# Hybrid Fourier and RWKV-7 layer: the pair scores as one sequence beside twelve column tiles, and eight modulation blocks in pieces

## The chip, the cores and the metric

The kernel runs on one core of a Trainium2 chip. The metric is the device time of the whole kernel in microseconds (us), as a median of runs; lower is better. Engines are named as in the profile: PE multiplies matrices (PEld is its weight load), DVE, ACT and POOL work on vectors, and DMA queues (SP's above all) move data between HBM and the on-chip memory. All data is float32.

## The reference

One layer of a backbone: a modulated norm, one input projection whose columns feed a Fourier mix and eight bidirectional RWKV-7 heads, an output projection, a second modulated norm and a gated MLP with a 3x3 grid convolution. There are 1024 latent tokens and 256 context tokens, and the width is 1024. What this change touches is the modulation, the projection and what the heads' scan reads:

```python
mod_x = jax.nn.silu(c) @ ada_w[l] + ada_b[l]
mod_c = jax.nn.silu(c_ctx) @ ada_w[l] + ada_b[l]
sh1, sc1, g1, sh2, sc2, g2 = [m[:, None, :] for m in jnp.split(mod_x, 6, axis=-1)]
...
h = modulate(rms_norm(x, norm1_g[l]), sh1, sc1)
hc = modulate(rms_norm(ctx, norm1_g[l]), sh1c, sc1c)
...
u = h @ w_in
...
rkv = conv1d_centred(u[..., :3 * RWKV_W], conv_w)
r, k, v = jnp.split(rkv, 3, axis=-1)
...
decay = jnp.exp(-jnp.exp(-jax.nn.softplus(-w_lora) - 0.5))
a = jax.nn.sigmoid((a0 + jnp.einsum("btdr,drc->btdc", ad, a2)).astype(jnp.float32))
kk = (k * k_k).astype(jnp.float32).reshape(b, t, N_HEADS, HEAD)
kk = kk * lax.rsqrt(jnp.sum(kk * kk, axis=-1, keepdims=True) + KK_EPS)
...
def step(s, inp):
    r_t, k_t, v_t, kk_t, a_t, w_t = inp
    sa = jnp.einsum("dbhij,dbhj->dbhi", s, kk_t)
    s = (s * w_t[..., None, :] - sa[..., :, None] * (kk_t * a_t)[..., None, :]
         + v_t[..., :, None] * k_t[..., None, :])
    y = jnp.einsum("dbhij,dbhj->dbhi", s, r_t) if readout else None
    return s, y
```

The kernel computes the scan in chunks of 64 tokens. The scores of a chunk are products of its decayed k, kk, a and r rows, and do not need v.

## The kernel before

**Column tiles.** The projection is computed in tiles of 128 columns, each over all tokens. A float32 product is made of three fast matmuls: weights and activations are split into a high and a low part (`whi`, `wlo`, `hTh`, `hTl`; L188, L189), and whi x hTh, whi x hTl and wlo x hTh are added up. A tile has eight steps over the 1024 rows of the weights (`product_part`, L197), each of six matmuls of 512 columns for the latent tokens (`plat`); k and v tiles then have 24 matmuls of 256 columns for the context tokens (`pctx`). Tile numbers m: r is 0 to 3, k is 4 to 7, v is 8 to 11, one for each pair of heads; 12 is wd (decay), 13 is ad (learning rate), 14 is gd (gate).

**Modulation.** silu(c) times the 1024 x 6144 modulation matrix is made in twelve blocks of 512 columns. Each block loads 2 MB (`load_ad`, two buffers `ad`), runs 32 matmuls on the 32-column `sc32` (`ada_rows`, L283, 64 in the profile since a float32 matmul takes two passes), copies the sums on ACT (`br`, L286) and, where they are needed by column, transposes them on PE (`ada_cols`, L292). The first norm needs four blocks, which come first. The other eight (gate 1, shift 2, scale 2 into `g1`, `sh2`, `G2`, and gate 2 into `modrow`) are needed only behind the scan.

**First stage.** `stage0` normalizes the tokens in three blocks (512, 512 and 256 tokens), and after each runs its part of the tiles 12 and 13.

**Stage 1a.** Then the tiles k, v and r of pair 0 and the tile gd. Behind each tile, `tick(1000)` runs all side work to its end, and two of the eight modulation blocks follow.

**Stage 1b.** A pair's work is the generator `pair(p)`: ten units, which are five blocks of 256 tokens, the context block first, in two directions. Per block, `lora` loads the rows of wd and ad (`wa`, L521) and of k, kk, v and r (`kvb`, L524), which went to DRAM as `kvd`, runs four matmuls (L533) and tanh (L536). Per unit, `parts` makes `kd`, `bk` and `x8` on ACT, POOL and DVE (L554 to L575), `scores` runs 8 matmuls (16 passes, L617), a masked copy on DVE (L619), 8 transposes (L627) and a store to `xd` (L631); `bonus` (L581 to L584) follows each latent block's second unit. Behind a k tile, `norms` makes kk: a square on ACT (L460), three matmuls that sum over heads, a logarithm (L464), an exponential (L466), a product on DVE (L467). Behind a v tile, `turns` transposes v in six pieces (L493) and stores them.

**Order.** These generators stand in a round-robin list `sides`. After each step of a tile over the latent tokens, `tick(rate)` with rate 2 advances two of them by one yield; `paced` holds a tile's matmuls behind the instruction that the tick four before gave. So the written order is the order on the engines, up to what the tile framework's priorities move. Pair p runs beside the tiles r, k and v of pair p+1, and pair 3 beside two Fourier tiles. After the three tiles `drain(g)` runs the pair to its end without tiles. Four PSUM banks `aux` serve lora, scores, transposes, norms and turns, and the context part of the tiles.

## Time and profile before

| | |
|---|---|
| median of three runs | 1780.15 us (1778.44 to 1785.54) |
| the profiled execution | 1789.06 us |
| its span, first to last instruction | 1787.3 us |
| PE busy | 1543.1 us, 86% of the span |
| PE weight loads | 1253.2 us, beside the matmuls |
| DVE busy | 1145.7 us, 64% |
| ACT busy | 678.6 us, 38% |
| POOL busy | 511.1 us, 29% |
| mean granted PE clock | 0.91 |
| read from and written to HBM | 178.52 MB and 66.33 MB |

Busy times are shares of the whole span, and the stages differ much from each other, so a stage has to be read by itself. Rows of the trace have a start or a count, the engine, the line in the kernel, the operation and its tiles (out<-in); in brackets stands the idle time of the engine ahead of the instruction, and what ended it. A row of busy time by stretch has the stretch in us from the span's start, its length, for each engine the busy time with the number of instructions, and then the granted PE clock (1.00 is full speed), the busy share of the DMA engines and the GB/s that they moved. PE busy at a low clock counts for less work than at a high one.

### The profile page before, as it was taken

The numbers are of one execution on the slowest core, as the hardware profiler recorded it, in microseconds if no ns is written. First come the engines' busy times: TensorE is split into PE (matmuls) and PEld (weight loads), VectorE is DVE, ScalarE is ACT, GpSimd is POOL, SyncE is SP. The second block draws the span as 40 slices with busy tenths as digits, with TensorE's granted clock in tenths as the row PEclk, the third lists the DMA queues.
The fourth block names the chain that finished last, engine by engine and source line by source line (L and its number), as shares of the span: only waits on it lengthen the run. The fifth ranks groups of instructions, "written<-read, shape, count | busy, mean of one in ns | idle before, by whom it ended". The sixth has DMA issues, their size and how long they took to land. (4 is left out here: it accounts for less than half of the span.)

```text
span 1787.3 us, 28924 instructions
## 1 busy us (share of the span) xinstructions
PE 1543.1 (86%) x11642; PEld 1253.2 (70%) x11642; DVE 1145.7 (64%) x1624; ACT 678.6 (38%) x1165; POOL 511.1 (29%) x443
## 2 busy tenths in 40 slices
PE   3896788888987766868888899999999999899996
PEld 2785566666766556657677788888888887687685
DVE  3611364748477754849355769999999999714613
ACT  3431345555543223321455542222222223434533
POOL 0021343535232114121211412222222223355354
PEclk7898798989986857869998999999999999899998
DMA  8348475757578589985671031111111113544542
GB/s 302 143 167 274 141 247 168 236 182 253 183 198 195 101 132 196 171 190 114 151 160 50 16 123 47 48 47 48 49 55 50 48 48 105 205 138 128 190 130 95
DMA packets 177750, 246.80 MB, mean 138 GB/s; under 512 B 52278, under 2 KB 115392, under 8 KB 177616
## 3 DMA queue, kind: packets, MB, share of 16 engines
q1 hardware_dynamic: 171440, 234.44, 45.9%
q0 software_dynamic: 6176, 10.51, 2.5%
q8 instruction: 92, 1.51, 0.4%
q14 instruction: 42, 0.34, 0.1%
HBM read 178.52 MB, written 66.33 MB: 137 GB/s over the span
## 5 line engine op out<-in xcount | busy, mean ns | idle before, releaser
L189 POOL TENSOR_TENSOR wlo<-wraw,whi 128x1024 fp32r<-128x1024 f32 x105 | 253.7, 2417 | 694.8 <-ACT whi L188 694.8
L1186 DVE SCALAR_TENSOR_TENSOR conv<-u,c_fcw,conv 128x945 f32<-128x945 f32 (+2 forms) x344 | 411.4, 1219 | 36.3 <-ACT conv L1179 20.9
L188 ACT ACTIVATE whi<-wraw 128x1024 fp32r<-128x1024 f32 x123 | 129.4, 1052 | 312.7 <-issue 166.7
L197 PE MATMUL u<-h2l,whi 128*128 128x512 f32 x672 | 207.2, 389 | 0.0
L197 PE MATMUL u<-h2h,wlo 128*128 128x512 f32 x672 | 207.1, 389 | 0.0
L197 PE MATMUL u<-h2h,whi 128*128 128x512 f32 x672 | 207.0, 389 | 0.0
L189 DVE TENSOR_TENSOR al<-act,ah 128x256 fp32r<-128x256 f32 (+1 forms) x88 | 62.4, 713 | 139.4 <-ACT ah L188 139.2
L197 PEld LDWEIGHTS u<-h2h,wlo 128*128 128x128 f32 x672 | 126.2, 188 | 26.1
L197 PEld LDWEIGHTS u<-h2l,whi 128*128 128x128 f32 x672 | 126.2, 188 | 26.1
L197 PEld LDWEIGHTS u<-h2h,whi 128*128 128x128 f32 x672 | 126.2, 188 | 26.0
L1243 PE MATMUL e<-wlo,ah 128*128 128x512 f32 x264 | 103.1, 391 | 2.8 <-POOL wlo L189 2.8
L1243 PE MATMUL e<-whi,al 128*128 128x512 f32 x264 | 103.1, 390 | 0.0
L197 PE MATMUL plat<-hTh,whi 128*128 128x512 f32 x272 | 99.8, 449 | 1.6 <-ACT whi L188 1.1
L188 ACT ACTIVATE ah<-act 128x256 fp32r<-128x256 f32 (+1 forms) x88 | 45.8, 523 | 140.3 <-PE e L1243 99.3
L197 PE MATMUL plat<-hTl,whi 128*128 128x512 f32 x272 | 91.7, 417 | 0.0
L197 PE MATMUL plat<-hTh,wlo 128*128 128x512 f32 x272 | 90.6, 412 | 1.0 <-POOL wlo L189 1.0
L887 POOL COPY WV<-SV 64x512 f32<-64x512 f32 x40 | 28.4, 709 | 189.3 <-PE py L953 89.7
L617 PE MATMUL aux<-x,bk 64*128 64x128 f32 (+1 forms) x640 | 59.8, 322 | 20.0 <-DVE bk L565 12.3
L617 PEld LDWEIGHTS aux<-x,bk 64*128 64x128 f32 x640 | 50.9, 222 | 36.7 <-issue 14.5
L561 POOL TENSOR_TENSOR kd<-kd,kvb 128x256 f32<-128x256 f32 x40 | 36.3, 918 | 108.5 <-DMA wa<-wad 49.5
L1243 PE MATMUL e<-whi,ah 128*128 128x512 f32 x264 | 67.0, 389 | 0.0
L197 PEld LDWEIGHTS plat<-hTl,whi 128*128 128x128 f32 x272 | 54.4, 201 | 13.1 <-issue 0.4
(291 smaller groups left out, 3152.4 us busy)
## 6 DMA issues: line engine op xcount, KB each, us to landing
wraw<-wd SPq DMA_DIRECT2D x66, 512.0 KB
xd<-x SPq DMA_DIRECT2D x32, 1024.0 KB
ad<-ada SPq DMA_DIRECT2D x12, 2048.0 KB
wraw<-wu SPq DMA_DIRECT2D x42, 512.0 KB
xs<-xd SPq DMA_DIRECT2D x16, 896.0 KB
xs<-xd SPq DMA_DIRECT2D x16, 640.0 KB
kvb<-kvd SPq DMA_DIRECT2D x16, 512.0 KB
wraw<-wi SPq DMA_DIRECT2D x15, 512.0 KB
```

Of the source, the lines that this page charges most:

```text
L188: self.nc.scalar.activation(hi, x, AF.Copy)
L189: (lo_eng or self.nc.gpsimd).tensor_sub(lo, x, hi.bitcast(F32))
L197: mm = self.nc.tensor.matmul(ps[:, b:b + n], wt[:, k, :], xt[:, k, b:b + n], start=k == 0 and i == 0, stop=k == 7 and i == 2)
L561: nc.gpsimd.tensor_mul(kd, kd, k)
L617: i = nc.tensor.matmul(ps[h][:, c, :64 * w], bk(c, h), x[R[h], c, 1:6 * w - 4:6], start=True, stop=True)
L887: nc.gpsimd.tensor_copy(wv[r, h], sv[r, h])
L1186: nc.vector.scalar_tensor_tensor(og[:, R, Cc], ug[:, Ri, Ci], self.fcw[:, m, w:w + 1], og[:, R, Cc], op0=OP.mult, op1=OP.add)
L1243: nc.tensor.matmul(t, x[:, 128 * (i - i0):128 * (i - i0) + 128], w[:, j, 512 * (b - b0):512 * (b - b0) + 512], start=k == 0 and m == 0, st ...
```

## The change

- The eight later modulation blocks become a generator, `ada_rest`. It issues its first two loads ahead of the first norm. One block runs behind each of the first two token blocks of that stage, and from then on the generator stands in `sides`: each block is written between steps of the tiles k, r and v of pair 0, with seven yields behind it, and not behind a tile. What is left behind the third tile is drained. The tiles that hold the results are allocated earlier.
- The tile gd goes from stage 1a to the beginning of stage 1b, beside pair 0. The order of the tiles is k, r, v in place of r, k, v (k, v, r for pair 0).
- The four pairs become one generator, `pairs`, that is drained only behind the Fourier tiles. A pair may begin when its own kk is stored (`("k", p)` in `have`): it then runs the context block's lora and the parts of its first two units. It goes on to the scores when its v is stored (`("v", p)`), and until then each turn of it yields without an instruction. So it begins beside the tiles r and v of its own pair.
- The context block's `kvb` load takes k and kk alone (two rows in place of three); v is used by the latent blocks' bonus only.

The core of the diff:

```diff
@@ -280,8 +280,8 @@
             for g in range(4):
-                nc.tensor.matmul(pm[32 * g:32 * g + 32, :128], self.sc32[:, j, :], ad[:, j, 128 * g:128 * g + 128],
-                                 start=j == 0, stop=j == 7)
+                self.rows_mm = nc.tensor.matmul(pm[32 * g:32 * g + 32, :128], self.sc32[:, j, :], ad[:, j, 128 * g:128 * g + 128],
+                                                start=j == 0, stop=j == 7)
         br = self.wa.tile([128, 128], F32, name="br", bufs=2)
@@ -300,13 +300,15 @@
             setattr(self, n, t)
+        self.G2, self.sh2, self.g1 = [self.const.tile([128, 8], F32, name=n) for n in ("G2", "sh2", "g1")]
+        self.modrow = self.dram.tile([1, D], F32, name="modrow")
         self.ones = self.const.tile([128, 128], F32, name="ones")
...
-    def stage0(self, wk, hT, first):
+    def stage0(self, wk, hT, first, rest):
@@ -381,6 +383,7 @@
                         nc.tensor.matmul(o, wt[:, k, :], xt[:, k, b:b + w], start=k == 0 and i == 0, stop=k == 7 and i == 2)
+            next(rest)
         return [[(ul, slice(0, T)), (uc, slice(T, TT))] for ul, uc in us]
@@ -389,7 +392,6 @@
             setattr(self, n, self.load(n))
-        self.G2, self.sh2, self.g1 = [const.tile([128, 8], F32, name=n) for n in ("G2", "sh2", "g1")]
@@ -400,7 +402,6 @@
         dram = self.dram.tile
-        self.modrow = dram([1, D], F32, name="modrow")
         self.sgd = dram([128, T], F32, name="sgd")
@@ -449,7 +450,7 @@
     def post_k(self, us, m):
-        nc, wk, pp = self.nc, self.wk, self.pp
+        nc = self.nc
         p = m - 4
@@ -459,23 +460,25 @@
             for b, n in BLOCKS:
-                aux = pp.tile([128, 512], F32, name="aux")
+                aux = self.pp.tile([128, 512], F32, name="aux")
                 i = nc.tensor.matmul(aux[:, :n], self.bones, kk[:, b:b + n], start=True, stop=True)
...
                     nc.sync.dma_start(self.kvd[p][:, 1], kk)
+                    self.have.add(("k", p))
                 yield i
...
     def post_v(self, us, m):
-        nc, wk, pp = self.nc, self.wk, self.pp
+        nc, wk = self.nc, self.wk
         p = m - 8
...
         nc.sync.dma_start(self.kvd[p][:, 2], v)
+        self.have.add(("v", p))
         rows = self.vd[:, :, p].rearrange("(b p) h d c -> d h p b c", p=128)
@@ -488,7 +491,7 @@
                     vt = wk.tile([128, 4, 128], F32, name="vt", bufs=2)
-                    aux = pp.tile([128, 512], F32, name="aux")
+                    aux = self.pp.tile([128, 512], F32, name="aux")
                     for b in range(nb):
@@ -520,7 +523,7 @@
             kv = wx.tile([128, 4, 256], F32, name="kvb", bufs=2)
-            n = 4 if H < 4 else 3
+            n = 4 if H < 4 else 2
             nc.sync.dma_start(kv[:, :n], self.kvd[p][:, :n, hs])
@@ -584,10 +587,15 @@
-        yield lora(blocks[0])
+        mm = lora(blocks[0])
         parts(*units[0])
+        yield mm
         for n, (H, d) in enumerate(units):
-            if n < 9:
+            if not n:
+                parts(*units[1])
+                while ("v", p) not in self.have:
+                    yield mm
+            elif n < 9:
                 parts(*units[n + 1])
@@ -596,6 +604,13 @@
                 next(self.first, None)
+
+    def pairs(self):
+
+        for p in range(4):
+            while ("k", p) not in self.have:
+                yield self.pace[-1]
+            yield from self.pair(p)
@@ -777,6 +792,17 @@
+    def ada_rest(self):
+
+        ads = deque(self.load_ad(4 + g) for g in range(2))
+        yield
+        for g in range(8):
+            i = self.ada_block(g, ads.popleft())
+            if g < 6:
+                ads.append(self.load_ad(6 + g))
+            for _ in range(7 if g > 1 else 1):
+                yield i
+
     def ada_block(self, g, ad):
@@ -785,11 +811,12 @@
                 nc.sync.dma_start(self.modrow[:, o + 128 * i:o + 128 * i + 128], br[32 * i:32 * i + 1, :])
-            return
+            return self.rows_mm
         o = (self.g1, self.sh2, self.G2)[g // 2]
...
             nc.vector.scalar_tensor_tensor(self.G2, self.G2, 1.0, self.n2g, op0=OP.add, op1=OP.mult)
+        return self.rows_mm
@@ -1285,7 +1312,7 @@
         b.xs, b.svs, b.zs, b.po, b.loads = {}, {}, {}, {}, []
-        b.sides, b.pace, b.rate, b.link = deque(), [], 2, None
+        b.sides, b.pace, b.rate, b.link, b.have = deque(), [], 2, None, set()
         solver, tail = ExitStack(), ExitStack()
@@ -1297,22 +1324,18 @@
                 b.stage0_open()
+                rest = b.ada_rest()
                 with ExitStack() as s0:
-                    us = b.stage0(pool("s0", s0), hT, (12, 13))
+                    us = b.stage0(pool("s0", s0), hT, (12, 13), rest)
                 b.wk = pool("s1", s1)
...
                 b.post_ad(us[1], 13)
-                ads = deque((g, b.load_ad(4 + g)) for g in range(2))
-                for m, post in ((4, b.post_k), (8, b.post_v), (0, b.post_r), (14, b.post_gd)):
+                b.sides.append(rest)
+                for m, post in ((4, b.post_k), (0, b.post_r), (8, b.post_v)):
                     post(b.project(hT, m), m)
-                    b.tick(1000)
-                    for _ in range(2):
-                        g, ad = ads.popleft()
-                        b.ada_block(g, ad)
-                        if g < 6:
-                            ads.append((g + 2, b.load_ad(6 + g)))
+                b.drain(rest)
             with s1:
@@ -1325,18 +1348,13 @@
                 b.first = b.solve(0)
-                for p in range(4):
-                    g = b.pair(p)
-                    b.sides.append(g)
-                    if p < 3:
-                        for m, post in ((1 + p, b.post_r), (5 + p, b.post_k), (9 + p, b.post_v)):
-                            post(b.project(hT, m), m)
-                    else:
-                        b.rate = 2
-                        b.fourier_open()
-                        us = b.fourier_first(hT)
-                    b.drain(g)
-                b.rate = 2
+                pairs = b.pairs()
+                b.sides.append(pairs)
+                for m, post in ((14, b.post_gd),) + tuple((m + p, post) for p in (1, 2, 3) for m, post in ((4, b.post_k), (0, b.post_r), (8, b.post_v))):
+                    post(b.project(hT, m), m)
+                b.fourier_open()
+                us = b.fourier_first(hT)
+                b.drain(pairs)
                 b.tick(1000)
```

The rows below are the order of the instructions in the built programs; a line number is that of the program the row is from, and x2 is a run of equal rows. First PE, ahead of pair 0. Before, the last four modulation blocks stand in a row, and the next tile (`plat_1464`, r of pair 1) comes behind them:

```order
L283 MATMUL aux_1221<-ad_1119,sc32_86 32x128 x32
L292 MATMUL aux_1256<-c_ident_76,br_1254 128x128
L283 MATMUL aux_1261<-ad_1159,sc32_86 32x128 x32
L292 MATMUL aux_1296<-c_ident_76,br_1294 128x128
L283 MATMUL aux_1361<-ad_1259,sc32_86 32x128 x32
L283 MATMUL aux_1400<-ad_1300,sc32_86 32x128 x32
L197 MATMUL plat_1464<-hTh_63,whi_1460 128x512 x2
L197 MATMUL plat_1464<-hTl_64,whi_1460 128x512 x2
```

In the changed program such a block stands inside the tile of k for pair 0 (`plat_841`), with the transpose of the block ahead of it (`br_881`) between the tile's steps:

```order
L197 MATMUL plat_841<-hTh_63,whi_837 128x512 x2
L292 MATMUL aux_883<-c_ident_76,br_881 128x128
L197 MATMUL plat_841<-hTl_64,whi_837 128x512 x2
L197 MATMUL plat_841<-hTh_63,wlo_838 128x512 x2
L197 MATMUL plat_841<-hTh_63,whi_837 128x512 x2
L197 MATMUL plat_841<-hTl_64,whi_837 128x512 x2
L197 MATMUL plat_841<-hTh_63,wlo_838 128x512 x2
L283 MATMUL aux_906<-ad_775,sc32_90 32x128 x32
L197 MATMUL plat_841<-hTh_63,whi_837 128x512 x2
```

Six of the eight blocks stand between tile matmuls in this manner, the last of them inside the tile v, and the other two stand in the first norm's stage. The first score of pair 0 stands inside the tile gd.

Next PE again, where pair 1 begins. Before, v of pair 1 is turned (L493), then comes pair 1's first lora (L533), and the tile under way is the r of pair 2 (`plat_2257`):

```order
L493 MATMUL aux_2265<-c_ident_76,v_2243 128x128 x4
L533 MATMUL aux_2284<-wa_2276,w2_2273 128x256
L533 MATMUL aux_2285<-wa_2276,w2_2273 128x256
L533 MATMUL aux_2284<-wa_2276,w2_2273 128x256
L533 MATMUL aux_2285<-wa_2276,w2_2273 128x256
L197 MATMUL plat_2257<-hTh_63,whi_2253 128x512 x2
L197 MATMUL plat_2257<-hTl_64,whi_2253 128x512 x2
L197 MATMUL plat_2257<-hTh_63,wlo_2254 128x512 x2
```

In the changed program the first lora of pair 1 (L536) stands inside its own r tile (`plat_2066`), one sum of kk (L464) ahead of it:

```order
L197 MATMUL plat_2066<-hTh_63,whi_2062 128x512 x2
L197 MATMUL plat_2066<-hTl_64,whi_2062 128x512 x2
L464 MATMUL aux_2122<-kk_2059,c_bones_800 128x256
L197 MATMUL plat_2066<-hTh_63,wlo_2063 128x512
L536 MATMUL aux_2145<-wa_2137,w2_2134 128x256
L197 MATMUL plat_2066<-hTh_63,wlo_2063 128x512
L536 MATMUL aux_2146<-wa_2137,w2_2134 128x256
L536 MATMUL aux_2145<-wa_2137,w2_2134 128x256
L536 MATMUL aux_2146<-wa_2137,w2_2134 128x256
L197 MATMUL plat_2066<-hTh_63,whi_2062 128x512 x2
```

The lora has moved ahead of r's and v's tiles; the first scores of pair 1 (L632) come only behind the whole v tile.

Last DVE, around v of pair 1 in the changed program (`r_2211` and `v_2296` are the convolutions, `bk_2172` is made for pair 1's second unit, `x8_2158` is its first unit's output, `kvb_2319` its first latent block):

```order
L568 TENSOR_TENSOR bk_2172<-al_2144,pi_2176 128x4x2x64
L449 SCALAR_TENSOR_TENSOR r_2211<-plat_2066,c_cw_784,r_2211 128x1023
L447 SCALAR_TENSOR_TENSOR v_2296<-plat_2222,c_cw_784,v_2296 128x1023
L449 SCALAR_TENSOR_TENSOR v_2296<-plat_2222,c_cw_784,v_2296 128x1023
L447 SCALAR_TENSOR_TENSOR v_2296<-pctx_2271,c_cw_784,v_2296 128x255
L449 SCALAR_TENSOR_TENSOR v_2296<-pctx_2271,c_cw_784,v_2296 128x255
L557 SCALAR_TENSOR_TENSOR cs_2407<-c_rst_1332,sg_2321 128x256
L557 SCALAR_TENSOR_TENSOR cs_2482<-c_rst_1332,sg_2322 128x256
L634 TENSOR_TENSOR x8_2158<-aux_2352,c_mask_804 128x4x64
L634 TENSOR_TENSOR x8_2158<-aux_2353,c_mask_804 128x4x64
L565 SCALAR_TENSOR_TENSOR al_2323<-al_2323,kvb_2319 128x256
L566 SCALAR_TENSOR_TENSOR x8_2406<-kvb_2319,P0_1334 128x4x64
```

The products `bk` of the first two units now stand around r's convolution (L449), ahead of v's, and the first instruction that reads the rows loaded behind v's store (`al_2323`, L565) stands behind the masks of the first unit (L634). In the program of before, the `bk` of both units stands behind v's convolution, and ahead of the first mask stands also what is read from the second block's rows.

## The prediction

> **What bounds the kernel now.** I read the page first, for the span and for the bytes moved over time. Then I cut the front part of the program into stretches at events that I can find again afterwards, and last I read single rows inside them.
>
> ```profile
> span 1787.3 us, 28924 instructions
> ...
> GB/s 302 143 167 274 141 247 168 236 182 253 183 198 195 101 132 196 171 190 114 151 160 50 16 123 47 48 47 48 49 55 50 48 48 105 205 138 128 190 130 95
> ```
>
> The profiled execution took 1789.06 us: 1787.3 us of span and 1.8 us around it. That is 0.5% above the median of the three runs, 1780.15 us. The sum is made against the profiled execution and its difference is then taken from the median.
>
> ```profile
> core 0: us, PE busy (x) PEld busy (x) DVE busy (x) ACT busy (x) POOL busy (x), PEclk, DMA share, GB/s
> 89.90:145.00 55.10, 54.07 (x372) 44.89 (x373) 11.83 (x14) 17.61 (x23) 11.93 (x5) 1.00 0.58 200
> 145.00:191.00 46.00, 27.82 (x419) 22.91 (x418) 3.08 (x8) 4.99 (x11) 2.35 (x1) 0.74 0.68 228
> 191.00:203.60 12.60, 8.46 (x31) 5.45 (x30) 3.16 (x8) 3.76 (x10) 2.49 (x4) 0.73 0.54 167
> 203.60:264.90 61.30, 52.55 (x358) 36.90 (x358) 43.13 (x68) 30.71 (x75) 30.92 (x40) 0.89 0.63 212
> 264.90:316.60 51.70, 43.61 (x245) 33.92 (x242) 22.53 (x33) 27.27 (x52) 17.85 (x18) 0.87 0.51 157
> 316.60:373.00 56.40, 48.86 (x325) 35.03 (x325) 35.46 (x53) 27.37 (x62) 23.81 (x29) 0.91 0.66 226
> 373.00:410.10 37.10, 31.97 (x183) 24.06 (x181) 21.55 (x30) 21.46 (x45) 14.88 (x17) 0.91 0.62 186
> 410.10:463.40 53.30, 46.67 (x325) 33.88 (x325) 34.65 (x53) 26.38 (x61) 21.06 (x28) 0.94 0.65 226
> 463.40:502.70 39.30, 36.10 (x224) 27.93 (x222) 21.91 (x34) 22.62 (x50) 11.52 (x15) 0.96 0.62 191
> 502.70:551.30 48.60, 35.98 (x270) 28.08 (x270) 43.91 (x87) 21.43 (x55) 19.55 (x27) 0.79 0.74 225
> 551.30:1787.30 1236.00, 1103.36 (x8464) 916.03 (x8464) 858.30 (x1146) 437.18 (x663) 349.51 (x255) 0.93 0.42 107
> ```
>
> In this view of busy time by stretch, 89.9 us is the first matmul of the tile of k for pair 0, 203.6 us the first score of pair 0, and 551.3 us the end of pair 3's scores. The four long stretches from 203.6 us are the bodies of the pairs. The three between them (51.7, 37.1 and 39.3 us) are the crossings, from the last scores of a pair to the third unit of the next. PE busy times granted clock is about the PE work at full speed. From 89.9 to 203.6 us it is 54.1 + 20.6 + 6.2 = 80.9 us of 113.7. In the bodies it is 46.8 + 44.5 + 43.9 + 28.4 = 163.6 of 219.6, in the crossings 37.9 + 29.1 + 34.7 = 101.7 of 128.1. No other engine is full there: DVE is the nearest, with 43.91 us of 48.6 in the last body.
>
> ```profile
> 552.16 0.52 SPq L631 DMA_DIRECT2D xd<-x  x1
> 556.63 0.51 SPq L886 DMA_DIRECT2D SV<-vd  x1
> ```
>
> The rows of the DMA queue show that the next stage begins its loads behind pair 3's last store, so the 1236 us after 551.3 move as a block with what is saved ahead of them. The change touches nothing there.
>
> **Part A: up to the first score of pair 0.**
>
> ```profile
> 125.12 1.96 PE L283 MATMUL aux<-ad,sc 128*32 128x128 f32 x64
> ...
> 166.10 3.64 PE L283 MATMUL aux<-ad,sc 128*32 128x128 f32 x64 [5.31 <-DMA ad<-ada]
> 170.19 0.47 PE L292 MATMUL aux<-c_ident,br 128*128 128x128 f32 x1 [0.45 <-ACT br L286]
> 172.27 3.46 PE L283 MATMUL aux<-ad,sc 128*32 128x128 f32 x64 [1.61 <-DMA ad<-ada]
> ```
>
> Before, four modulation blocks in a row wait for their 2 MB loads, 6.2 us from one to the next, and each costs 3.5 us on a cold PE against 1.96 us when it stands between tile matmuls. The change puts two blocks into the stage of the first norm and six between the matmuls of k, r and v, and takes the tile gd out of this part.
>
> ```profile
> 102.53 0.28 PE L197 MATMUL pctx<-hTh,whi 128*128 128x256 f32 x1
> 102.65 0.28 PE L197 MATMUL pctx<-hTl,whi 128*128 128x256 f32 x1
> ...
> 142.03 0.62 PE L197 MATMUL plat<-hTl,whi 128*128 128x512 f32 x2
> 142.48 0.62 PE L197 MATMUL plat<-hTh,wlo 128*128 128x512 f32 x2
> ...
> 246.90 1.16 PE L617 MATMUL aux<-x,bk 64*128 64x128 f32 x16
> 247.89 0.41 PE L627 MATMUL aux<-c_ident,bk 64*128 64x64 f32 x8
> ...
> 407.48 1.14 PE L533 MATMUL aux<-wa,w 64*128 64x256 f32 x8
> ```
>
> These rows give the prices at full clock, from start to start: 0.45 us for two matmuls of 512 columns, 0.12 us for one of 256, 1.0 us for a unit's scores, 0.34 for its transposes, 1.06 for a lora group. So gd, 24 steps of two matmuls, is 24 x 0.45 = 10.9 us. PE work left in part A: 80.9 - 10.9 - 2 x 1.96 - 1.5 (half of v's turns, which now run beside the pair) = 64.6 us. That is the lower end, with all loads in time.
>
> The other end is the transfers. The three rows hold 55.1 x 0.200 + 46.0 x 0.228 + 12.6 x 0.167 = 23.6 MB. One block's load (2.1) comes earlier now, and v, its rows and gd (0.7 + 1.3 + 0.5, from the tiles' shapes) go out later: 19.0 MB stay. At the 302 GB/s of the page's first slice this takes 63 us, at the 228 of the waiting stretch 83, at the 200 of the first row 95. Blocks stand in PE's order, so a late load stops the tiles behind it. I take 250 GB/s, between the first two, as two loads may be in flight but each waits for a buffer: 76 us, plus 2 us for the two blocks in the earlier stage, where PE has idle time. **Part A: 113.7 to 78, so -36** (ends -47 and -17).
>
> **Part B: from there to the end of pair 3.** Before, a crossing is made so:
>
> ```profile
> 287.51 0.61 SPq L478 DMA_DIRECT2D kvd<-v  x1
> ...
> 292.32 1.04 SPq L524 DMA_DIRECT2D kvb<-kvd  x2
> 296.48 1.82 POOL L561 TENSOR_TENSOR kd<-kd,kvb 128x256 f32<-128x256 f32 x2 [2.19 <-DMA kvb<-kvd]
> 300.72 1.98 PE L617 MATMUL aux<-x,bk 64*128 64x64 f32 x16 [8.09 <-DVE bk L565]
> ```
>
> From the store of v to the first scores are 13.2 us, with nothing for PE at the end of it (8.09 us idle, then 1.98 us for what takes 1.16 warm). The change loads only k and kk for the first block, so pair 1's first two units are made ready while r's and v's tiles run, some 17 us of pure PE work (24 + 8 steps of 0.45 plus 24 of 0.12). Only the third unit still waits for v. Of the crossings' 128.1 - 101.7 = 26.4 us without work I take 20 as saved. What stays: DVE makes pair 1's bk ahead of the second half of r's convolution, and it reads the loaded v ahead of the second unit's mask, so behind these waits stand a PSUM bank and then PE. By the same round trip of 4.8 + 4.2 us (287.51 to 292.32 to 296.48), v is there some 11 us after its convolution, while the first two units keep PE busy for about 14.
>
> What is added: gd's 10.9 us beside pair 0, whose body has 61.3 - 46.8 = 14.5 us without work. I put +5; the ends are 0 and 10.9. The wider sequence also mixes the sums of kk with the pair's own activations, and the table of functions is switched 16 times there instead of 8:
>
> ```profile
> L464 ACT ACT_TABLE_LOAD x4 | 5.1, 1283 | 0.1
> L466 ACT ACT_TABLE_LOAD x4 | 5.1, 1283 | 0.1
> ```
>
> Eight more at 1.283 us are 10.3 us of ACT, in the bodies of pairs 1 and 2, where ACT is busy 27.37 of 56.4 us and 26.38 of 53.3. I put 0 on the path; the other end is 10.3. The load of two rows of the context block instead of three spares 0.13 MB a pair, which I count as nothing; the no-op turns of a waiting pair issue nothing. The tile work beside the bodies hardly moves: by the order, 90 matmuls of 512 columns stand beside pair 0's (before 86), 72 beside pairs 1 and 2 (before 77), 42 beside pair 3's (before 36). **Part B: -20 + 5 = -15** (ends: -26 if all idle in the crossings goes and gd hides; +13 if the crossings yield 8 us, gd hides nowhere and every switch is on the path).
>
> The Trainium skill, "ScalarE: Activation LUTs", section "What ACT_TABLE_LOAD costs", gives 1283 ns for the load and a drain of 1380 ns with it, 2.66 us a switch. The load agrees with the rows; a drain is not seen in them (0.1 us idle ahead of four loads). By the page eight switches would be 21.3 us, and with all of them on the path the sum would be 30 us instead of 51.
>
> **Sum:** -36 - 15 = -51 us. The profiled span would be 1736, and 1780 - 51 = **1729 us** the median.
>
> **Rivals.**
> 1. *The loads set the pace of part A.* At 200 GB/s it takes 95 + 2 us and saves 17 instead of 36: 1748 us. For it: the stretch from 89.9 us moved no more. Against it: half of that stretch asked for no block. Chance 0.18.
> 2. *PE closes up everywhere.* If bodies and crossings reach the share of the last crossing, 34.7 of 39.3 (88%), the work of 265.3 + 10.9 us takes 313 us instead of 347.7, part B is -35 and the time 1709; with part A at its lower end 1698. For it: PE works in its order, and more independent work stands between the waits. Against: in the last body DVE is full. Chance 0.22.
> 3. *The switches of the activation table lie on the path.* Each of the eight delays a tanh or an exponential that the next unit's scores need: 10.3 us, 1739. Chance 0.08 beside the forecast's own range.
> 4. *Slower.* The third unit's load holds DVE ahead of the second unit's mask. The masks hold PSUM banks, four in all, so PE stops behind it, at three crossings and at pair 0's start. The cover is the 14 us of two units. With a round trip of 9 us nothing is lost; at 25 us, when blocks, stores and tile weights share the queue, each place loses 15 to 16 us beyond today's, 4 x 16 = 64, and 1729 + 64 = 1793. It decides from some 24 us on, 10 more than v's 13.2 us from store to scores now. Chance 0.04.
> 5. *No change:* part A yields 17 and part B gives 13 back: 1776. Chance 0.04.
>
> **How the numbers follow.** The forecast has 0.44, and its own range is 1712 to 1745. The range of 1695 to 1755 takes in rivals 1, 2 and 3 and leaves out the last two and the far ends. About 0.5%, 9 us, is what a measurement can tell from no change here. Faster by more than that holds for the forecast and rivals 1 to 3: 0.91, with a little of each at their ends; 0.05 within, 0.04 slower.
>
> **What would show it.** Part A: the last modulation block ends near 150 us instead of 189, and PE's idle time for ad falls below 10 us behind the first norm. If it stays above 20, rival 1 holds. First scores near 168 us. Part B: no wait of 8 us ahead of the first scores of pairs 1 and 2, crossings near 45, 32 and 37 us, bodies as long as now, and the granted clock of the crossings above 0.95. Pair 3's scores end near 500 us. If PE waits for the second unit's mask while DVE waits for kvb, rival 4's mechanism is there, whatever its size. If the stage after pair 3 is no longer 1236 us, the block did not move as a block, and the sum is wrong in a place that I did not look at.

## The result, and the profile after

| | before | after | ratio, 95% interval |
|---|---|---|---|
| median of four runs | 1781.25 us (1778.44 to 1785.54) | 1750.99 us (1750.46 to 1753.65) | 0.9831 [0.9808, 0.9854] |
| the same two kernels again, 11 and 5 runs | 1785.07 us | 1746.75 us | 0.9795 [0.9773, 0.9818] |
| profiled execution | 1789.06 us | 1751.00 us | |

The change makes the kernel faster, by 30 us in the first comparison and 38 in the second; 51 were forecast. The profiled execution of before lay 7.8 us above its median, so the two traces differ by 38 us.

The page of the changed kernel, span and GB/s by slice:

```profile
span 1749.2 us, 28932 instructions
...
GB/s 315 188 289 205 241 174 176 226 220 210 198 214 123 167 147 176 152 183 128 180 95 36 42 97 49 49 49 49 49 49 49 49 49 160 176 124 129 195 130 96
```

Busy time by stretch, cut at the same events as before (90.9 us: first matmul of k for pair 0; 142.1: end of the last modulation block; 163.9: first score of pair 0; then body, crossing, body and so on, to the end of pair 3's scores at 514.15):

```profile
90.90:142.10 51.20, 50.26 (x573) 40.72 (x570) 8.97 (x15) 14.75 (x20) 8.43 (x4) 1.00 0.85 308
142.10:163.90 21.80, 17.32 (x79) 12.41 (x76) 8.68 (x14) 9.62 (x22) 6.39 (x7) 0.92 0.61 180
163.90:231.00 67.10, 56.95 (x402) 40.98 (x401) 42.04 (x68) 35.02 (x79) 32.02 (x38) 0.92 0.66 220
231.00:276.90 45.90, 42.96 (x240) 33.41 (x238) 22.40 (x31) 23.06 (x48) 15.49 (x17) 0.96 0.57 180
276.90:334.40 57.50, 47.62 (x320) 34.62 (x319) 36.26 (x53) 36.05 (x67) 24.73 (x29) 0.88 0.66 220
334.40:372.20 37.80, 31.71 (x188) 24.13 (x188) 21.71 (x30) 18.29 (x43) 12.63 (x16) 0.91 0.59 181
372.20:428.70 56.50, 48.47 (x320) 34.19 (x319) 34.79 (x53) 35.17 (x66) 21.46 (x28) 0.88 0.61 210
428.70:466.90 38.20, 35.71 (x228) 27.69 (x228) 21.57 (x34) 19.19 (x44) 10.53 (x15) 1.00 0.60 185
466.90:514.15 47.25, 35.14 (x276) 27.00 (x276) 44.78 (x90) 23.08 (x58) 19.08 (x27) 0.86 0.77 233
514.15:1749.20 1235.05, 1107.22 (x8464) 919.14 (x8464) 857.29 (x1144) 437.95 (x663) 349.81 (x255) 0.92 0.42 107
```

The reader is to see three things. **Ahead of the first score** the stretch went from 113.7 us to 73.0, and begins 1.0 later: 39.7 us gained. While the blocks run, PE is busy 50.26 of 51.2 us at full clock, and 308 GB/s come in. **From there to the end of pair 3** it takes 350.25 us, against 347.7 before: 2.5 us lost. The crossings are 121.9 us (before 128.1), the bodies 228.4 (before 219.6). **Behind pair 3** 1235 us are left, as before. So all of the gain is in the first part. Some of it is work that moved: 105 tile steps of two matmuls stood ahead of the first score before, and 87 stand there now. The other 18, about 8 us at 0.45 us each, are in the second part.

Where the second part's time may have gone is seen in what DVE waited for. Two rows of the waits of DVE between pair 0's first score and pair 3's last, of the kernel before (us in total, times, longest):

```profile
DVE cs L554 <- ACT sg L538: 21.3, 9, 6.4
...
DVE al L562 <- DMA kvb<-kvd: 3.6, 5, 2.0
```

and the same two of the changed kernel:

```profile
DVE cs L557 <- ACT sg L541: 37.6, 15, 6.7
DVE al L565 <- DMA kvb<-kvd: 17.0, 7, 5.6
```

These two grew by 29.7 us, but others fell, among them the wait for the exponential of kk, from 19.6 us to 8.3, and in all DVE waits 123.2 us before and 125.8 after. So the rows name suspects and prove nothing; the experiments have to decide. PE's own waits in that stretch add up to 51.8 us before and 51.4 after. The 12.3 us for `bk` ahead of a pair's first scores became 0.7. In their place stand 12.3 us ahead of v's turns:

```profile
PE aux L496 <- DVE vrev L491: 12.3, 4, 5.8
```

The longest of these waits is at pair 2. DVE's timeline there (start, duration, instruction; in brackets idle time and what ended it):

```profile
358.68 0.42 DVE L565 SCALAR_TENSOR_TENSOR al<-al,kvb 128x256 f32<-128x256 f32 x1 [5.64 <-DMA kvb<-kvd]
...
361.84 0.74 DVE L634 TENSOR_TENSOR x<-aux,c_mask 128x256 f32<-128x256 f32 x2
363.21 0.49 DVE L578 SCALAR_TENSOR_TENSOR bt<-kvb,c_rk__794,bt 128x256 f32<-128x256 f32 x1 [0.64 <-POOL bt L577]
363.62 0.42 DVE L491 COPY vrev<-v 128x512 f32<-128x512 f32 x1
```

PE's timeline at the same place:

```profile
350.46 1.11 PE L632 MATMUL aux<-x,bk 64*128 64x64 f32 x16 [0.28 <-DVE v L449]
...
355.69 1.11 PE L632 MATMUL aux<-x,bk 64*128 64x64 f32 x16
...
357.76 0.61 PE L197 MATMUL plat<-hTh,wlo 128*128 128x512 f32 x2
364.18 1.09 PE L496 MATMUL aux<-c_ident,vrev 128*128 128x128 f32 x4 [5.80 <-DVE vrev L491]
...
366.84 1.05 PE L197 MATMUL plat<-hTl,whi 128*128 128x512 f32 x2
```

SP's queue:

```profile
350.38 0.33 SPq L480 DMA_DIRECT2D kvd<-v  x1
...
353.94 1.25 SPq L527 DMA_DIRECT2D kvb<-kvd  x2
```

v's store goes out at 350.38, the load that reads it at 353.94, and DVE has the rows at 358.68: 8.3 us for the round trip. DVE takes the third unit's `al` first in its order. The second unit's mask and the reversed copy do not read the loaded rows, but they stand behind it. PE has work for 8 us from the first score on (350.46 to 358.4), and then stops. The stop costs more than its 5.80 us: two matmuls of 512 columns take 0.61 us ahead of it and 1.05 us behind it.

The other wait is ACT's. Its timeline in the body of pair 1, where the norm of pair 2's k runs beside the scores:

```profile
291.96 0.69 ACT L465 ACTIVATE kk<-aux,epskk 128x512 f32<-128x512 f32 x1
292.67 1.28 ACT L539 ACT_TABLE_LOAD   x1
293.97 0.48 ACT L539 ACTIVATE sg<-aux,c_w 128x256 f32<-128x256 f32 x1
...
296.65 1.28 ACT L465 ACT_TABLE_LOAD   x1
297.94 0.69 ACT L465 ACTIVATE kk<-aux,epskk 128x512 f32<-128x512 f32 x1
298.53 0.59 ACT L563 ACTIVATE kd<-al,ka,kah 128x256 f32<-128x256 f32 x1
299.14 1.28 ACT L559 ACT_TABLE_LOAD   x1
300.43 0.42 ACT L559 ACTIVATE P<-cs 128x256 f32<-128x256 f32 x1
300.75 0.40 ACT L560 ACTIVATE pi<-cs 128x256 f32<-128x256 f32 x1
301.17 1.28 ACT L465 ACT_TABLE_LOAD   x1
```

Logarithm, tanh, logarithm, exponential, logarithm: each turn loads a table. Behind them DVE waits, 6.68 us for the first scan:

```profile
295.87 0.69 DVE L557 TENSOR_TENSOR_SCAN cs<-c_rst,sg 128x256 f32<-128x256 f32 x1 [6.68 <-ACT sg L541]
...
299.15 0.43 DVE L565 SCALAR_TENSOR_TENSOR al<-al,kvb 128x256 f32<-128x256 f32 x1 [1.74 <-ACT kd L563]
300.88 0.42 DVE L566 SCALAR_TENSOR_TENSOR x<-kvb,P 128x256 f32<-128x256 f32 x1 [1.30 <-ACT P L559]
```

### The profile page after: what moved, and what is told of

Same layout as the page of the kernel before. It is cut to its first block, busy times and chain, and to the rows that moved or that the text cites. A ratio compares the mean times of both kernels' runs of the same rounds, so it can differ in the third digit from the quotient of the medians.

```text
span 1749.2 us, 28932 instructions
## 1 busy us (share of the span) xinstructions
PE 1532.3 (88%) x11642; PEld 1241.5 (71%) x11642; DVE 1144.9 (65%) x1624; ACT 690.9 (39%) x1173; POOL 506.9 (29%) x443
## 5 line engine op out<-in xcount | busy, mean ns | idle before, releaser
L188 ACT ACTIVATE ah<-act 128x256 fp32r<-128x256 f32 (+1 forms) x88 | 45.9, 523 | 140.1 <-PE e L1270 99.4
L197 PE MATMUL plat<-hTl,whi 128*128 128x512 f32 x272 | 90.9, 416 | 0.0
L197 PEld LDWEIGHTS plat<-hTh,whi 128*128 128x128 f32 x272 | 47.9, 198 | 23.2 <-issue 15.0
L197 PEld LDWEIGHTS plat<-hTh,wlo 128*128 128x128 f32 x272 | 53.9, 199 | 13.8 <-DVE wlo L664 0.9
L557 DVE TENSOR_TENSOR_SCAN cs<-c_rst,sg 128x256 f32<-128x256 f32 x40 | 30.6, 764 | 48.6 <-ACT sg L541 44.2
## 6 DMA issues: line engine op xcount, KB each, us to landing
wraw<-wd SPq DMA_DIRECT2D x66, 512.0 KB, 3.5
wraw<-wu SPq DMA_DIRECT2D x42, 512.0 KB, 3.4
kvb<-kvd SPq DMA_DIRECT2D x16, 512.0 KB, 4.7
wraw<-wi SPq DMA_DIRECT2D x15, 512.0 KB, 5.1
```

The costliest lines, as they stand in the source:

```text
L188: self.nc.scalar.activation(hi, x, AF.Copy)
L197: mm = self.nc.tensor.matmul(ps[:, b:b + n], wt[:, k, :], xt[:, k, b:b + n], start=k == 0 and i == 0, stop=k == 7 and i == 2)
L557: nc.vector.tensor_tensor_scan(cs, self.rst, o(sg), 0.0, op0=OP.mult, op1=OP.add)
```

## The experiments

The theory: the gain comes from the modulation pieces; the one sequence would bring its share too, but two waits of DVE took it back, the one for the load behind v's store and the one for activations behind table loads. Two measures are given for each run: the ratio to the kernel before on the same chip, and the stretch from the first to the last start of the scores' matmuls, from one trace. These two rows give it, before (345.5 us) and after (348.1):

```profile
L617 PE MATMUL aux<-x,bk x640: 269/273/580, 203.6 to 549.1; 64*128 64x128 f32 x128, 64*128 64x64 f32 x32
```

```profile
L632 PE MATMUL aux<-x,bk x640: 269/272/579, 163.9 to 512.0; 64*128 64x128 f32 x128, 64*128 64x64 f32 x32
```

The stretch is the sharper measure where the same tiles stand in it: the two traces of the changed kernel give 348.1 and 348.3 us. What lies behind pair 3 has the same work in all of these kernels and took 1227 to 1241 us. Where the tile gd stands ahead of the first score (before, pieces only, the old loop and both runs with gd first), the stretch is shorter by what gd costs in it.

| run | ratio, 95% interval | scores, us from to | us |
|---|---|---|---|
| pieces only | 0.9846 [0.9812, 0.9880] | 183.5 to 525.1 | 341.6 |
| sequence only | 0.9983 [0.9962, 1.0004] | 197.4 to 545.0 | 347.6 |
| gd first | 0.9832 [0.9799, 0.9864] | 181.6 to 522.0 | 340.4 |
| v apart | 0.9743 [0.9707, 0.9778] | 163.8 to 498.4 | 334.6 |
| after, again | 0.9795 [0.9773, 0.9818] | 166.1 to 514.4 | 348.3 |
| norms whole | 0.9744 [0.9722, 0.9766] | 166.2 to 500.6 | 334.4 |
| vd stores on ACT | 0.9831 [0.9801, 0.9860] | 165.7 to 518.2 | 352.5 |
| wait for r | 0.9720 [0.9704, 0.9735] | 164.8 to 503.2 | 338.4 |
| one logarithm | 0.9744 [0.9713, 0.9775] | 165.7 to 497.4 | 331.7 |
| v apart and norms whole | 0.9651 [0.9626, 0.9677] | 166.8 to 488.2 | 321.4 |
| old loop, v apart | 0.9794 [0.9770, 0.9819] | 180.0 to 516.4 | 336.4 |
| both mends, gd first | 0.9678 [0.9656, 0.9700] | 176.4 to 492.7 | 316.3 |

**Which part brings the gain.** The first run takes the pieces into the kernel of before, with its loop over pairs. It also drops the `tick(1000)` behind each tile, as the change does; stage 1a is then

```diff
+                b.sides.append(rest)
                 for m, post in ((4, b.post_k), (8, b.post_v), (0, b.post_r), (14, b.post_gd)):
                     post(b.project(hT, m), m)
-                    b.tick(1000)
...
+                b.tick(1000)
```

> The modulation pieces alone, in the old loop over pairs (order k, v, r, gd in stage 1a). Theory T (nearly all of the gain comes from the modulation blocks; the one sequence gives back what it takes): 1781 - 27 = about 1754, and in the trace the last block ends about 142 us and the first score of pair 0 stands about 175 us, 28 earlier than before (gd's 10.9 us stay ahead of it). Rival S (the sequence brings its forecast 15 and the pieces less than the one profile of before shows): 1764 to 1768.

The second takes the sequence alone:

```diff
+                for m, post in ((4, b.post_k), (0, b.post_r), (8, b.post_v), (None, None)):
+                    if post:
+                        post(b.project(hT, m), m)
+                        b.tick(1000)
+                    for _ in range(2):
+                        g, ad = ads.popleft()
+                        b.ada_block(g, ad)
```

> The one sequence of pairs alone, with the modulation blocks two behind each tile as before (the last two behind the third). Theory T: 1781 to 1777, no gain beyond 4 us; from the first score of pair 0 to the end of pair 3 it takes about 350 us as in the changed kernel. Rival S: 1781 - 15 = 1766, and the same stretch takes 335 us or less.

The pieces alone brought 1.5%, 27 us of 1786; the sequence alone 0.2%, with an interval that reaches to no change. Theory T held. The gain of the pieces includes what the missing `tick(1000)` gives, since the norm and the turns of pair 0 now stand between tile steps too; no run parts the two. The first score came at 183.5 us, not at 175: the forecast of 28 us earlier left out that v's turns stay in stage 1a there too, with 3.7 us in which PE waits for their stores, and the last block ended at 161 us, not at 142. In the traces the last scores come 24 us earlier with the pieces alone, 4 with the sequence alone and 35 to 37 with the whole change, so 7 to 9 us belong to neither alone.

**The tile gd.**

```diff
-                for m, post in ((4, b.post_k), (0, b.post_r), (8, b.post_v)):
+                for m, post in ((4, b.post_k), (0, b.post_r), (8, b.post_v), (14, b.post_gd)):
                     post(b.project(hT, m), m)
...
-                for m, post in ((14, b.post_gd),) + tuple((m + p, post) for p in (1, 2, 3) for m, post in ((4, b.post_k), (0, b.post_r), (8, b.post_v))):
+                for m, post in tuple((m + p, post) for p in (1, 2, 3) for m, post in ((4, b.post_k), (0, b.post_r), (8, b.post_v))):
```

> The changed kernel with the tile gd back in stage 1a, behind v, with the sequence and the pieces kept. By the forecast's own term (gd costs 5 of its 10.9 us beside pair 0) it is 6 us slower: 1757. Theory T' (PE is short of work nowhere beside pair 0, so gd costs its 10.9 us in either place): within 2 us of 1751.

The ratio is that of the changed kernel in the first comparison, as T' had it, and 0.4% above that of the second (0.9795), as the forecast's own term had it. In the trace the last scores stand at 522.0 us, against 512.0 and 514.4 in the two traces of the changed kernel. But this order also has 40 table loads where the changed kernel has 38, so the 8 to 10 us need not be gd's alone. The same move was made on the kernel with both mends, which are told below.

> Both mends, with the tile gd back in stage 1a. With gd moved alone the trace had the end of pair 3's scores 8 to 10 us later than the changed kernel, while the times could not tell them apart. If gd beside pair 0 is worth what that trace shows: end of pair 3's scores 8 to 10 us later than with both mends (488.2), ratio 0.970. If gd costs its 10.9 us in either place: within 3 us of 488.2, ratio 0.965.

There the last scores came 4.5 us later, with 30 table loads in both, and the ratio went from 0.9651 to 0.9678, with intervals that overlap. Neither expectation held clearly. The traces suggest that gd is partly hidden beside pair 0, by some 4 us where the loads are equal, but two traces of one kernel differed by 2.4 us there; the times do not show it.

**The wait for v.** `kvd` gets the rows k, kk, r, v, and v is loaded by itself:

```diff
-            kv = wx.tile([128, 4, 256], F32, name="kvb", bufs=2)
-            n = 4 if H < 4 else 2
+            kv = wx.tile([128, 3, 256], F32, name="kvb", bufs=2)
+            n = 3 if H < 4 else 2
             nc.sync.dma_start(kv[:, :n], self.kvd[p][:, :n, hs])
+            if H < 4:
+                vb = wx.tile([128, 256], F32, name="vb", bufs=2)
+                nc.sync.dma_start(vb, self.kvd[p][:, 3, hs])
```

> The changed kernel with v as the last row in DRAM and loaded by itself, so that the products for the first latent block wait for k, kk and r only and not for v's store. Theory K (DVE waits for the load behind v's store, 2.5 and 5.6 us at pairs 1 and 2, ahead of the second unit's mask and the reversed copy for v's turns, and PE waits for these, 12.3 us at four places): the 12.3 us fall below 5 and the time is 1743 to 1747. Rival Q (the queue: v's turns wait for their buffers, whose stores stand behind the loads on SP's queue, and 16 more loads make that worse): 1751 to 1756, with the same waits of PE for the reversed copy.

The time fell by more than expected, the stretch by 13.5 us, with the table loads still at 38. DVE's wait for the rows went from 17.0 to 3.3 us:

```profile
DVE al L570 <- DMA kvb<-kvd: 3.3, 1, 3.3
```

PE's waits for the reversed copy fell from 12.3 to 8.3 us only, so this part of the expectation missed; PE's waits in all fell from 51.4 to 42.1. What DVE waits for ahead of the reversed copy is now the stores of v's turns, 9.6 us where the changed kernel had 3.0:

```profile
DVE vrev L491 <- DMA vd<-vt: 9.6, 4, 3.6
```

So with the first wait gone the buffers of rival Q are felt. Whether the queue had a share in the first wait was asked on the changed kernel, with the stores of v's turns on another queue:

```diff
-                        nc.sync.dma_start(rows[d, h, :, t0:t0 + nb], vt[:, :nb, 64 * h:64 * h + 64])
+                        nc.scalar.dma_start(rows[d, h, :, t0:t0 + nb], vt[:, :nb, 64 * h:64 * h + 64])
```

> The changed kernel with the stores of v's turned pieces on ACT's queue instead of SP's. Theory Q (the reversed copies wait for buffers whose stores stand behind the load that waits for v's store): PE's waits for the reversed copy fall from 12.3 to below 5 us, 5 to 8 us faster. Theory K (DVE itself waits for that load, with the copies queued behind): at least 9 us of them stay, within 3 us.

They stayed, at 13.7 us, as K had it and not Q; the stretch grew by 4 us and the ratio by 0.4%, somewhat more than K's 3 us. The same move together with v loaded by itself, where the stores are waited for, was not run. Then the wait was moved from v to r, with the first latent block's bonus put behind the second's, so that four units need no v:

```diff
+                while ("r", p) not in self.have:
+                    yield mm
+            elif n == 4:
                 while ("v", p) not in self.have:
                     yield mm
+                load_v(0)
+                load_v(3)
+                parts(*units[n + 1])
```

> As with v loaded by itself, and a pair goes on to its scores when its r is stored; only from the fifth unit on does it wait for v, and the first latent block's bonus comes with the second's. Theory K: the units that wait for nothing new stand beside v's tile, so the round trip behind v's store has no one waiting; 2 to 6 us faster than with v loaded by itself (0.974 of before), about 0.971. Rival R (the round trip behind r's store takes its place at the same distance): 0.974 to 0.98, with PE's waits ahead of the third unit as long as with v.

The ratio, 0.972, is about what K gave, but the stretch is 338.4 us, 4 longer than with v loaded by itself. This order also has only 30 table loads, which is worth some 14 us by the runs that follow; against the run with both mends (321.4), which has 30 too, it is 17 us worse. PE now waits at other places, 10.5 us for the squares of kk and 7.4 us for `bk`. So the wait for r brings nothing of its own, but R's wait ahead of the third unit is not shown to be the reason.

```profile
PE aux L464 <- ACT kk L461: 10.5, 3, 4.1
```

**The table loads.** The norm as one yield, so that its three logarithms stand together:

```diff
                     self.have.add(("k", p))
-                yield i
+            yield i
```

> The changed kernel once more, unaltered, beside the next three: ratio 0.983 to the kernel before as at first. In the trace, first score of pair 0 at 164 us and the end of pair 3 at 515 us again within 2 us; the part behind it may differ by some us with the granted clock (1232 to 1239 us in the six executions so far).

> The changed kernel with the sum of kk as one yield, so that its three logarithms stand together on ACT (30 table loads as before the change, not 38). Rival 3 of the prediction (the eight loads lie on the path): 5 to 10 us faster than the changed kernel, and PE's waits for kk (8.0 us there, 3.5 before) fall to 4. Other view (ACT has room, 190 of 350 us busy): within 3 us.

The changed kernel came out at 0.9795, lower than the expected 0.983, with intervals that overlap; its stretch was the same again. Against it the whole norm brought 0.9744, and the stretch 348.3 us became 334.4, so the time bears out rival 3 of the prediction. DVE's wait for the activations `sg`, 37.6 us in the changed kernel, fell, but its wait for the exponential of kk rose by as much, from 8.3 us:

```profile
DVE cs L557 <- ACT sg L541: 27.5, 16, 3.7
DVE kk L468 <- ACT kk L467: 18.5, 3, 8.8
```

So these rows do not show through which wait the time was won. PE's waits in all fell from 51.4 us to 43.6. Its wait for the squares stayed at 5.9 us; that for ACT's logarithms (2.1) went. But this edit also moves the three sums on PE. So the same eight loads were taken away with the order on PE kept:

```diff
-                nc.scalar.activation(kk[:, b:b + n], aux[:, :n], AF.Ln, bias=self.epskk)
+                nc.scalar.activation(kk[:, b:b + n], aux[:, :n], AF.Copy)
                 if b == 1024:
+                    nc.scalar.activation(kk, kk, AF.Ln, bias=self.epskk)
```

> The changed kernel with the three sums of kk copied as they come, at the same three yields, and one logarithm over all 1280 columns at the last: 30 table loads in place of 38, the order on PE kept, three copies more a pair on ACT. Theory L (the eight loads, 10.3 us of ACT ahead of the activations that the scans wait for, are what the whole norm saves): ratio about 0.975 as with the whole norm, from pair 0's first score to pair 3's end about 337 us (348 with the change). Rival M (it is that the whole norm finishes kk earlier and puts the three sums at one place): as the changed kernel, 0.98 to 0.983 and 346 to 350 us.

331.7 us, although ACT has more to copy, and 30 table loads: rival M is out. Two different edits that share the eight loads give about the same, so it is the loads, or the turns between logarithms and the pair's activations that come with them. The wait through which they cost stays open, for here DVE's wait for `sg` fell only to 33.7 us:

```profile
DVE cs L558 <- ACT sg L542: 33.7, 14, 5.6
```

Eight loads of 1.283 us are 10.3 us of ACT, and without them the stretch is 13.9 and 16.6 us shorter, 1.7 to 2.1 us for each. How that can be more than the loads themselves is seen in PE's busy time from the first score to the end of pair 3's scores, for the changed kernel run again, the whole norm and the one logarithm:

```profile
166.10:516.60 350.50, 297.58 (x1965) 221.15 (x1965) 223.29 (x358) 189.79 (x402) 136.56 (x170) 0.92 0.64 207
166.20:502.80 336.60, 292.25 (x1966) 218.28 (x1966) 223.75 (x356) 178.64 (x394) 134.57 (x170) 0.93 0.67 215
165.70:499.60 333.90, 288.46 (x1964) 214.76 (x1964) 226.13 (x358) 182.25 (x397) 133.76 (x170) 0.95 0.67 217
```

PE is without work for 52.9, 44.4 and 45.4 us. So 8 us or so of each gain is time in which PE no longer stands, about 1 us a load, and the rest, 5 and 9 us, is the same matmuls at a higher granted clock (0.92, 0.93 and 0.95; busy time times clock is 272 to 274 us in all three). The Trainium skill, "ScalarE: Activation LUTs", section "What ACT_TABLE_LOAD costs", puts a switch at 2.66 us with a drain; the trace has no drain ahead of the loads shown above (291.96 + 0.69 = 292.65, and the load begins at 292.67).

**Both, and the old loop.**

> Both mends on the changed kernel. If they take away two different waits (DVE for the load behind v's store, DVE for ACT's activations behind table loads), each 13.5 to 14 us of the stretch from pair 0's first score to pair 3's end: 348 - 27 = 321 us there, ratio about 0.967. If both free the same stretch of DVE at the begin of a pair, they overlap: 330 us or more, ratio 0.972 or above.

The two add up: 321.4 us, 26.7 less than the changed kernel. With 0.9651 this is the fastest kernel of the study, 1725 us. To the end of pair 3's scores PE is without work for 37.7 us (51.7 with the change) and busy for 285.9 (298.5), at a granted clock of 0.95 instead of 0.91: half of the gain is waiting, and half is the clock. The rows are of the changed kernel and of this one:

```profile
163.90:514.10 350.20, 298.51 (x1964) 221.96 (x1964) 223.50 (x357) 189.86 (x402) 135.93 (x170) 0.91 0.64 207
166.80:490.40 323.60, 285.88 (x1965) 213.92 (x1965) 225.23 (x356) 178.48 (x394) 134.44 (x170) 0.95 0.69 224
```

DVE's waits for `sg` are 19.9 us there and for the rows 5.0:

```profile
DVE cs L562 <- ACT sg L545: 19.9, 14, 3.5
...
DVE al L570 <- DMA kvb<-kvd: 5.0, 1, 5.0
```

Would the old loop have gained as much from v apart? It was put on the run with pieces only, with the context block loading k and kk alone:

> The modulation pieces with the old loop over pairs, v loaded by itself and the context block without v. If the crossings of the old loop wait for v's round trip alone: the 13.5 us that PE waits for bk there go, ratio 0.9846 - 0.007 = 0.977, as much as with the sequence. If kk, stored 2 us ahead of v at pair 1, takes v's place: 2 to 3 us a crossing, 0.981, and then the sequence (0.974 with the same edit) is worth 0.7% that the old loop can't have.

It gained 5 us of the stretch (341.6 to 336.4), PE's wait for `bk` fell from 13.5 us to 6.2, and the ratio 0.9794 is nearer to the second expectation. The old loop has 30 table loads already, so the second mend has no loads to take away there. The sequence with both mends is 15 us shorter in the stretch and 1.4% faster in all.

## Why the prediction was right, and where it was not

The forecast was 1729 us. The 1750.99 us lie in the wide range, 1695 to 1755, but above the forecast's own, 1712 to 1745. What lies beyond 1745 was taken in for rival 1 (1748), a part A held up by its loads, which did not come. So the direction was right by part A, and that the time still lies in the range, with part B at nothing, is in part luck. Of the terms of the sum:

- **Part A, -36: right, -39.7.** Its two conditions are seen. The last block ends at 142.1 us (forecast near 150), and PE waits 0.9 us for `ad` behind the first norm, against 12.8 before. The transfers were priced at 250 GB/s and came at 308 up to the last block, 270 over all of part A, so rival 1 (200 GB/s) is out. The stages ahead cost 1.0 us instead of 2. Of gd's 24 steps 15 still stand ahead of the first score, while 9 steps of pair 1's r tile have left: 18 steps less in all, where the forecast took off 24.
- **Part B, -15: wrong, +2.5 in the trace, and 0.2% for the sequence alone.** Two steps failed. The first is "Of the crossings' 128.1 - 101.7 = 26.4 us without work I take 20 as saved": the crossings got 6 us shorter. The forecast was not of one piece here: its own signs, crossings near 45, 32 and 37 us, add up to 14 saved. They came at 45.9, 37.8 and 38.2, so the second, with the 5.80 us wait, is the one that missed. The old wait did go (`bk`, 12.3 to 0.7 us), but the sentence on its replacement had the cover wrong: "v is there some 11 us after its convolution, while the first two units keep PE busy for about 14". The round trip took 8.3 us from store to DVE, as counted or less, but at pair 2 the cover was 8 us, since the tile steps between two units are few and the mask of the second unit stands behind the wait. Loading v by itself brought 13.5 us.
- The second is "I put 0 on the path; the other end is 10.3" for the eight table loads, argued from ACT's share of the bodies. Without them the stretch was 13.9 and 16.6 us shorter, more than the end that was kept, of which some 8 us are waiting of PE and the rest its clock. ACT is half idle, but that does not keep its loads off the path; by which wait they get there stays open. The bodies, forecast "as long as now", got 8.8 us longer in all, 5.8 of it beside pair 0.
- **gd, +5.** 9 of its 24 steps, 4.1 us of work, stood behind the first score, with the 9 steps of pair 1's r tile; how much of it PE had to spare, the runs leave open.
- **The block behind pair 3** moved as a block: 1236 and 1235 us.
- **The difference to the median.** The sum was made against an execution that lay 7.8 us above its median. Of the 22 us between forecast and result, part B explains 17.5, that difference some 8, and part A gave 4 back.

With both waits taken away the stretch is 26.7 us shorter than with the change, 24 shorter than before: near the lower end given for part B (-26). The old loop with v loaded by itself lacks 15 of these. So the sequence can bring what was forecast of it, and its price was paid by two waits, which the prediction had both named: **rival 3** (switches, 0.08, priced at 10.3 us) and the mechanism of **rival 4** (third unit's load ahead of the second unit's mask, priced at up to 64 us). The latter was dismissed by its cover, and at 13.5 us it does not make the kernel slower, but it takes the gain away. Rival 2 (PE closes up everywhere) did not come.

## What to carry to other kernels

When two pieces of work are laid beside each other, look at every engine that both use, not only at the full one: an engine that is half idle still delays the path if a function switch or a wait comes in ahead of the instruction that the path needs. When a wait is taken away, the cover of the next one is what stands in program order between its issue and its first user on that engine, and it has to be counted row by row, with the instructions queued behind that user. A wait can cost more than its length: here about half of what two waits took was PE working on at a lower clock. A round trip through DRAM that only one late consumer needs should be a transfer of its own.

## What was not expected of the hardware

With the 2 MB modulation loads beside matmuls all transfers together reached 308 GB/s over 51 us, where the stretch of before had 200 to 228. PE's granted clock over the stretch of the scores went from 0.91 to 0.95 when 14 us of its waits went, and that was worth about as much as the waits. And programs with the same work behind pair 3 took 1227 to 1241 us there, with granted clocks of 0.97 to 0.99 in its middle part; a gain of a few us is read better from a stretch of the trace than from the whole time.
